# Two output projections as three products of split operands, and one pool of twelve for the ring's slots

## The chip, the cores and the metric

The kernel runs on one core of one Trainium2 chip, in one launch. The metric is the device time of that launch in microseconds. The core's engines run side by side, each through its own list of instructions in order: TensorE (PE, with its weight loads as PEld), VectorE (DVE), ScalarE (ACT), GpSimd (POOL) and SyncE (SP), which here issues nearly all the transfers from the chip's memory.

## The reference, cut to what matters

A two-layer network on 256 tokens of width 1024. Layer 0 mixes tokens by attention, layer 1 by a Hyena convolution; each mixer ends in an output projection, and a mixture of 16 experts follows it. Modulation vectors (`mod_w`, 40 MB) scale and shift around all of this.

```
def attention_group_mixer(...):          # layer 0
    ...
    def merge(oa, ow):
        ...
        cat = jnp.concatenate([oa..., ow...], -1)
        return cat @ w_out               # [256,1024] @ [1024,1024]

def hyena_mixer(h, w_in, ...):           # layer 1
    u = h @ w_in
    ...
        z = gate * (conv + zf32 * sk[o]).astype(h.dtype)
    return z @ w_out                     # [256,1024] @ [1024,1024]

def moe_ffn(h, router_w, router_bias, w_gate, w_up, w_down):
    scores = jax.nn.softmax(hf @ router_w)
    ...                                  # best group of 4, two experts a token
    def expert_block(args):
        xb, e = args
        return (jax.nn.silu(xb @ w_gate[e]) * (xb @ w_up[e])) @ w_down[e]
```

All inputs are float32.

## The kernel before, in words

**Weights and the ring.** Every weight tile is 1 MB, [128, 2048] float32. Twelve slots of that size, w0 to w11, make the ring; `slots["order"]` hands them out by turns, so each load has its slot fixed when the program is written, and waits until that slot's last reader is done. From the end of each mixer to the end of its experts there are also `MORE[l]` extra slots (4 in layer 0, 5 in layer 1). `load` (L146) issues every tile on SP's queue, in program order, with at most eight under way.

**Stages.** Layer 0's mixer streams the modulation weights beside attention. `mixer_tail` then runs: it loads the mod vector g1b and the first tiles of expert 0 into the extra slots, `project` (L427) multiplies mixT (or z2T in layer 1) by the four tiles of `out_weights`, `normalize` (L435, L436, L361, L375) adds the residual and takes the layer norm, `logits` (L445 to L453) transposes it and scores the experts, and a chain of small DVE steps makes the routing tables. `project` accumulates token half t in two PSUM banks, one for each 512 columns; a float32 matmul of 512 columns shows as two records in the trace.

**Experts.** `moe` takes the positions p = 0 to 9 in order: `up` (L648), `turn_mid` (L657), `down` (L667), `back` (L686), with two large experts as dense pieces (L711, L723) between p = 1 and 8. An expert needs 12 tiles: four pairs of gate and up, and four of down. At p = 9 (`NEST`) the kernel first loads eight tiles of expert 9 into ring slots of their own, then enters nested conditionals (`rare`, L761) for the experts at positions 10 to 13, which run only where the routing needs them, with the other slots; after them it loads expert 9's last four tiles and runs it.

**The end.** After layer 1's experts the kernel adds the last term, takes a layer norm (L1409, L1410) and stores the output.

**Split operands.** `split` writes `hi`, a rounded copy (ACT), and `lo`, the difference (DVE), as float32r; the Hyena input products (L1296) for five of six column blocks already use hi·hi, hi·lo and lo·hi in place of one float32 product.

Of the kernel before, what the change touches and what calls it, by code (L numbers as in the profile page):

```python
# [75 lines left out]
def emit(tc, I, O):  # L76
# [3 lines left out]

    with es:
        cp = es.enter_context(tc.tile_pool(name="cp", bufs=1))
        ring = es.enter_context(tc.tile_pool(name="ring", bufs=1))
        accp = es.enter_context(tc.tile_pool(name="accp", bufs=1, space=PSUM))
        miscp = es.enter_context(tc.tile_pool(name="miscp", bufs=1, space=PSUM))
        dram = es.enter_context(tc.tile_pool(name="dram", bufs=1, space=DRAM))
# [15 lines left out]
                mturn[0] ^= 1  # L102
            return miscp.tile([128, 512], F32, name=f"mis{i}", tag=f"mis{i}")

        slots = {"order": list(range(RING)), "at": 0}

        def wtile(i=None):

            if i is None:
                i = turns()[0]  # L110
                slots["at"] += 1
            return (ring if i < RING else slots["pool"]).tile([128, 2048], F32, name=f"w{i}", tag=f"w{i}")

        def turns(order=None):

            if order is None:
                a = slots["at"] % len(slots["order"])
                return slots["order"][a:] + slots["order"][:a]
            slots["order"], slots["at"] = order, 0

        def more_ring(l):

# [4 lines left out]
            return xp, pool_  # L127

        def all_slots(n):
            turns(turns() + [RING + i for i in range(n)])  # L130

        def less_ring(pool_):
            turns([i for i in turns() if i < RING])
            for p_ in pool_:
                p_.__exit__(None, None, None)

        def load(src, shape, slot=None):
            t = wtile(slot)
            v = t
            n = 1  # L140
            for s in shape:
                n *= s
            v = t[:, :n]
            if len(shape) == 2:
                v = v.rearrange("p (a b) -> p a b", a=shape[0])
            sp.dma_start(out=v, in_=src)  # L146
            return v
# [249 lines left out]
            dve.tensor_tensor(out=b, in0=b, in1=sh, op=ALU.add)  # L397

        def out_weights(src):
            return [load(src[256 * i:256 * i + 256, :].rearrange("(k p) n -> p k n", p=128), [2, 1024]) for i in range(4)]  # L400


        def stage_h2():
# [2 lines left out]
        def mixer_tail(l, stage, mixT, wout, R):  # L406
# [15 lines left out]
                pe.matmul(lg[0:16, 256:257], rw[:, kc, :], cb[:, kc:kc + 1], start=(kc == 0), stop=(kc == KC - 1))  # L422
            dve.tensor_copy(lcol[0:16, :], lg[0:16, 256:257])

            def project(t, banks, kh):
                for kc, hf in kh:
                    m = pe.matmul(banks[hf], mixT[:, kc, 128 * t:128 * t + 128], wout[kc // 2][:, kc % 2, 512 * hf:512 * hf + 512],  # L427
                                  start=(kc == 0), stop=(kc == KC - 1))
                return m.ins

            def normalize(t, banks):
# [142 lines left out]
        def expert_loads(l, idx, have=(), most=12, new=False):  # L574

            def src(nm, i):
                return expert_of(l, nm, idx)[256 * i:256 * i + 256, :].rearrange("(k p) f -> p k f", p=128)

            order = [(nm, i) for i in range(4) for nm in ("exp_w_gate", "exp_w_up")] + [("exp_w_down", i) for i in range(4)]
            ts = list(have)  # L580
            for nm, i in order[len(ts):]:
                ts.append(load(src(nm, i), [2, 1024], slot=RING + len(ts) if new else None))
                if len(ts) == most:
                    break
            return ts
# [144 lines left out]
        def moe(l, h2, R, first, filler):  # L730
            with tc.tile_pool(name=f"mp{l}", bufs=2, reuse_waits="tile") as mp:
# [73 lines left out]
                for p in range(RARE):  # L805
                    if p == NEST:

                        ix = number(1, place(p), [ET.SP], NE - 1)
                        w = expert_loads(l, ix, most=8)
                        last.back()  # L810
                        last = None
                        free = turns()
                        own, free = free[-8:], free[:-8]
                        turns(free)
                        rare(RARE)
                        E.bank = E.banks()
                        free.sort(key=lambda i: i < RING)
                        turns(free[:4])
                        E.w = expert_loads(l, ix, have=w)
                        turns(free[4:] + own + free[:4])  # L820
                    elif p == 0:
                        E.w = first
                    else:
                        ix = number(1, place(p), [ET.SP], NE - 1) if p > 1 else 1
                        E.w = expert_loads(l, ix, have=second if p == 1 else (), most=8)
                        if p in PIECES:
                            r, half, down = PIECES[p]
                            dw = dense_loads(l, number(1, 2 + r, [ET.SP], NE - 1), half, down)
                        E.w = expert_loads(l, ix, have=E.w)
                    E.up()  # L830
                    if last:
# [403 lines left out]
                if i + 1 < len(oq):  # L1235
                    spec_loads(*oq[i + 1])

        def win_tile(s, i):
            return load(wi[512 * i:512 * i + 512, 512 * s:512 * s + 512].rearrange("(k p) n -> p k n", p=128), [4, 512])

        with tc.tile_pool(name="fp", bufs=1, reuse_waits="tile", side="right") as fp:
            wi = I["hy_w_in"][0]
            moe(0, h2, R, first, filler)
            ws0 = [win_tile(j // 2, j % 2) for j in range(NAHEAD)]
        less_ring(rmore)

        R = routing_tables()
# [227 lines left out]
```

## Time and profile before

| | |
|---|---|
| median of 3 runs | 1320.58 us (1314.1 to 1323.14) |
| profiled execution | 1321.82 us, span 1320.1 us |
| mean granted TensorE clock | 0.946 |
| PE busy | 1177.6 us (89%) |
| DVE busy | 550.0 us (42%) |
| ACT busy | 216.6 us (16%) |
| moved by DMA | 443.88 MB, 336 GB/s on average |

The time of an execution is 1.7 us longer than its span here. A busy share is an average over stages: the same engine can be the limit in one stage and idle in the next, so each stage is read for itself.

### The profile page before, as it was taken

What the parts mean: (1) busy time and instruction counts of PE and PEld (TensorE: products, weight loads), DVE (VectorE), ACT (ScalarE), POOL (GpSimd) and SP (SyncE); (2) the same over time, 40 slices, a digit from 0 to 9 for tenths busy, and PEclk for the clock granted to TensorE, in tenths of its full rate; (3) what the DMA queues carried; (4) which work ended last, traced back from release to release, by engine and by line L of the source; (5) the groups of instructions that cost most, each with busy time, mean ns of one, the idle gap of its engine ahead of it and who ended that gap; (6) DMA issues with size and microseconds to landing.
All of it is one profiled execution on the core that took longest, in us unless ns stands there. A gap on an engine that the chain in (4) does not pass through costs nothing. (4 is left out here: it accounts for less than half of the span.)

```text
span 1320.1 us, 19948 instructions
## 1 busy us (share of the span) xinstructions
PE 1177.6 (89%) x8106; PEld 700.8 (53%) x8106; DVE 550.0 (42%) x1131; ACT 216.6 (16%) x431; POOL 48.4 (4%) x88
## 2 busy tenths in 40 slices
PE   5999989978999999999776779899799999999994
PEld 2444545434845648466432348675366465574842
DVE  2467998374122141321421157995530312313033
ACT  2133546130000000000000025321210000000000
POOL 1000000211000000000100010000100000000000
PEclk9999998978999999999977789899799999999998
DMA  9978986869599799999999794368499999999994
GB/s 329 397 287 318 336 328 234 319 260 394 217 405 405 267 397 405 408 398 392 398 395 409 275 372 159 127 225 334 180 393 408 401 390 359 402 374 402 408 383 160
DMA packets 133207, 443.88 MB, mean 336 GB/s; under 512 B 8271, under 2 KB 9895, under 8 KB 133104
## 3 DMA queue, kind: packets, MB, share of 16 engines
q1 hardware_dynamic: 127168, 426.76, 83.7%
q0 software_dynamic: 4864, 13.18, 2.9%
q10 hardware_dynamic: 1072, 2.54, 0.6%
q8 instruction: 68, 1.11, 0.3%
q14 instruction: 35, 0.29, 0.1%
HBM read 437.19 MB, written 5.26 MB: 335 GB/s over the span
## 5 line engine op out<-in xcount | busy, mean ns | idle before, releaser
L648 PE MATMUL acc<-w,xe 128*32 128x256 f32 (+1 forms) x2688 | 216.7, 428 | 17.9 <-PEq L761 7.4
L711 PE MATMUL acc<-xnT,w 128*128 128x256 f32 x1024 | 222.8, 379 | 0.4 <-DVE xs L692 0.4
L711 PEld LDWEIGHTS acc<-xnT,w 128*128 128x128 f32 x1024 | 194.3, 190 | 26.7 <-DVE xs L692 0.6
L648 PEld LDWEIGHTS acc<-w,xe 128*32 128x32 f32 (+1 forms) x2688 | 102.6, 120 | 121.4 <-issue 68.1
L667 PE MATMUL acc<-w,aT 128*32 128x256 f32 (+1 forms) x1344 | 120.2, 426 | 9.7 <-DMA w<-in_exp_w_down 3.9
L723 PE MATMUL acc<-w,hid 128*128 128x512 f32 x256 | 111.5, 593 | 0.3 <-DVE xs L692 0.3
L714 DVE TENSOR_TENSOR hid<-hid,acc 128x256 f32<-128x256 f32 x32 | 13.4, 420 | 190.4 <-ACT hid L713 190.4
L271 DVE SCALAR_TENSOR_TENSOR w<-w,cz,w 128x1024 f32<-128x1024 f32 x60 | 75.0, 1277 | 22.7 <-DMA w<-in_mod_w 22.6
L667 PEld LDWEIGHTS acc<-w,aT 128*32 128x32 f32 (+1 forms) x1344 | 48.4, 117 | 66.9 <-issue 30.0
L723 PEld LDWEIGHTS acc<-w,hid 128*128 128x128 f32 x256 | 48.0, 190 | 58.6 <-issue 57.6
L692 DVE TENSOR_TENSOR xs<-xs,acc 128x512 f32<-128x512 f32 x92 | 57.6, 683 | 47.1 <-PE acc L686 47.1
L652 DVE TENSOR_TENSOR ac<-ac,acc 128x256 f32<-128x256 f32 (+1 forms) x23 | 10.7, 467 | 148.3 <-PE acc L648 148.3
L943 PE MATMUL acc<-w,hT 128*128 128x512 f32 (+1 forms) x192 | 71.5, 523 | 0.9 <-DVE mr L166 0.8
L1296 PE MATMUL acc<-hTh,w 128*128 128x256 f32 x320 | 63.0, 293 | 5.4 <-DVE w L155 3.7
L1296 PEld LDWEIGHTS acc<-hTh,w 128*128 128x128 f32 x320 | 50.2, 190 | 9.7 <-DVE w L155 4.4
L725 DVE SCALAR_TENSOR_TENSOR do<-acc,wtP,g2b 128x512 f32<-128x512 f32 x32 | 24.0, 751 | 69.7 <-PE acc L723 69.7
L943 PEld LDWEIGHTS acc<-w,hT 128*128 128x128 f32 x192 | 35.4, 190 | 32.4 <-issue 29.2
L651 ACT ACTIVATE ac<-acc 128x256 f32<-128x256 f32 (+1 forms) x23 | 9.7, 420 | 254.9 <-PE acc L648 254.9
L616 PE MATMUL mis<-h,Pu 128*32 128x256 f32 (+1 forms) x336 | 38.1, 470 | 13.8 <-DVE Pu L610 9.9
L686 PE MATMUL acc<-xg,PT 32*128 32x256 f32 (+1 forms) x336 | 41.2, 434 | 6.0 <-DVE xg L672 4.6
L713 ACT ACTIVATE hid<-acc 128x256 f32<-128x256 f32 x32 | 12.3, 383 | 208.7 <-PE acc L711 208.7
L1296 PE MATMUL acc<-hTl,w 128*128 128x256 f32 x160 | 45.1, 283 | 0.0
(351 smaller groups left out, 1272.9 us busy)
## 6 DMA issues: line engine op xcount, KB each, us to landing
w<-in_exp_w_up SPq DMA_DIRECT2D x108, 1024.0 KB, 17.8
w<-in_exp_w_gate SPq DMA_DIRECT2D x108, 1024.0 KB, 17.7
w<-in_exp_w_down SPq DMA_DIRECT2D x108, 1024.0 KB, 10.8
w<-in_mod_w SPq DMA_DIRECT2D x40, 1024.0 KB, 9.6
w<-in_hy_w_in SPq DMA_DIRECT2D x12, 1024.0 KB, 13.8
w<-in_attn_w_in SPq DMA_DIRECT2D x9, 1024.0 KB, 13.1
w<-in_mod_w SPq DMA_DIRECT2D x16, 512.0 KB, 10.8
w<-in_attn_w_out SPq DMA_DIRECT2D x4, 1024.0 KB, 13.4
```

The source lines that it names most:

```text
L271: dve.scalar_tensor_tensor(out=st["acc"][:, k], in0=w[:, k], scalar=c_[k], in1=st["acc"][:, k], op0=ALU.mult, op1=ALU.add)
L616: pe.matmul(gb[S * j:S * j + S, 0:nn], Pu[:, t, 0:S], self.h2[:, t, nn * j:nn * j + nn], start=(t == 0), stop=(t == 1), tile_position=(0, ...
L648: pe.matmul(A[m][S * j:S * j + S, 0:nn], self.xe[:, kc, :], w[:, nn * j:nn * j + nn], tile_position=(0, S * j), start=(kc == 0), stop=(kc ...
L667: pe.matmul(y[S * q:S * q + S, 0:nn], lhs, w[:, nn * q:nn * q + nn], tile_position=(0, S * q), start=(kc == 0), stop=(kc == KC - 1))
L686: pe.matmul(o, self.PT[r, 128 * t:128 * t + 128], self.yb[r, 0:nn], start=True, stop=True, tile_position=(S * q, 0))
L692: dve.tensor_tensor(out=x_, in0=x_, in1=o, op=ALU.add)
L711: pe.matmul(b[:, N * m:N * m + N], ws[m][kc // 4][:, kc % 4, 128 * fb:128 * fb + 128], h2T[:, kc, :], start=(kc == 0), stop=(kc == KC - 1))
L714: dve.tensor_tensor(out=hid[:, fb, :], in0=hid[:, fb, :], in1=b[:, N:2 * N], op=ALU.mult)
L723: pe.matmul(b, hid[:, fb, 128 * t:128 * t + 128], ws[fb // 2][:, fb % 2, s_], start=(fb == 0), stop=(fb == 3))
L725: dve.scalar_tensor_tensor(out=o, in0=b, scalar=wt[:, t], in1=g2b[:, s_], op0=ALU.mult, op1=ALU.mult)
L943: pe.matmul(bank[:, 0:width], hT[:, kc, 128 * t:128 * t + 128], st["w"][kc // per][:, kc % per, :], start=(kc == 0), stop=(kc == KC - 1))
L1296: pe.matmul(b[:, 0:N], w_, m, start=(kc == 0 and i == 0), stop=(kc == KC - 1 and i == len(ps) - 1))
```

## The change

`out_weights` still loads four tiles, but each is split into a hi and a lo tile that take two more slots from the ring; mixT or z2T is split the same way, in four pieces, into mixH and mixL; `project` makes three float32r products for each block where it made one of float32. The ring becomes one pool of twelve buffers: a load takes whichever buffer the pool gives it. For expert 9 only `MORE[l]` tiles (4 in layer 0, 5 in layer 1) are loaded ahead of the conditionals, into the extra slots, so that the conditional experts have all twelve ring buffers; its other 8 (layer 0) or 7 (layer 1) tiles are loaded behind them.

```diff
@@ ring
-        ring = es.enter_context(tc.tile_pool(name="ring", bufs=1))
+        ring = es.enter_context(tc.tile_pool(name="ring", bufs=RING))
...
-            return (ring if i < RING else slots["pool"]).tile([128, 2048], F32, name=f"w{i}", tag=f"w{i}")
...
+                slots["turn"] = (slots["turn"] + 1) % (RING + slots["more"])
+                i = slots["turn"] - RING
+            if i < 0:
+                return ring.tile([128, 2048], F32, name="w", tag="w")
+            return slots["pool"].tile([128, 2048], F32, name=f"w{i}", tag=f"w{i}")
@@ out_weights
-            return [load(src[256 * i:256 * i + 256, :].rearrange("(k p) n -> p k n", p=128), [2, 1024]) for i in range(4)]
+
+            o = []
+            for i in range(4):
+                w = load(src[256 * i:256 * i + 256, :].rearrange("(k p) n -> p k n", p=128), [2, 1024])
+                hi, lo = (wtile().rearrange("p (k n) -> p k n", k=2) for _ in range(2))
+                for k in range(2):
+                    split(w[:, k], hi[:, k], lo[:, k])
+                o.append((hi, lo))
+            return o
@@ mixer_tail
+            mixH, mixL = (stage.tile([128, KC, N], F32, name=nm, tag=nm) for nm in ("mixH", "mixL"))
+            for t in range(2):
+                for c0 in range(0, KC, 4):
+                    v = mixT[:, c0:c0 + 4, 128 * t:128 * t + 128]
+                    split(v, mixH[:, c0:c0 + 4, 128 * t:128 * t + 128], mixL[:, c0:c0 + 4, 128 * t:128 * t + 128])
+
             def project(t, banks, kh):
                 for kc, hf in kh:
-                    m = pe.matmul(banks[hf], mixT[:, kc, 128 * t:128 * t + 128], wout[kc // 2][:, kc % 2, 512 * hf:512 * hf + 512],
-                                  start=(kc == 0), stop=(kc == KC - 1))
+                    wh, wl = (r_(w[:, kc % 2, 512 * hf:512 * hf + 512]) for w in wout[kc // 2])
+                    mh, ml = (r_(v[:, kc, 128 * t:128 * t + 128]) for v in (mixH, mixL))
+                    for i, (a_, b_) in enumerate(((mh, wh), (mh, wl), (ml, wh))):
+                        m = pe.matmul(banks[hf], a_, b_, start=(kc == 0 and i == 0), stop=(kc == KC - 1 and i == 2))
                 return m.ins
@@ moe, p == NEST
-                        w = expert_loads(l, ix, most=8)
+                        w = expert_loads(l, ix, most=MORE[l], new=True)
                         last.back()
                         last = None
-                        free = turns()
-                        own, free = free[-8:], free[:-8]
-                        turns(free)
                         rare(RARE)
                         E.bank = E.banks()
-                        free.sort(key=lambda i: i < RING)
-                        turns(free[:4])
                         E.w = expert_loads(l, ix, have=w)
-                        turns(free[4:] + own + free[:4])
...
+                        if p + 1 == NEST:
+                            all_slots(0)
                         E.w = expert_loads(l, ix, have=E.w)
@@ hyena
-            ws0 = [win_tile(j // 2, j % 2) for j in range(NAHEAD)]
+            ws0 = [win_tile(j // 2, j % 2, -1) for j in range(NAHEAD)]
```

In the changed kernel's lines `load` is L142, `split`'s subtraction L151, `project` L440, `normalize` L447, `logits` from L457.

Order on PE at the end of layer 0's projection, before: acc_1591 and acc_1592 are the banks of token half 0, acc_1593 and acc_1594 those of half 1.

```order
L427 MATMUL acc_1591<-w_1551,mixT 128x512
L427 MATMUL acc_1592<-w_1551,mixT 128x512
L427 MATMUL acc_1593<-w_1545,mixT 128x512 x2
L427 MATMUL acc_1593<-w_1547,mixT 128x512 x2
L427 MATMUL acc_1593<-w_1549,mixT 128x512 x2
L427 MATMUL acc_1593<-w_1551,mixT 128x512 x2
L427 MATMUL acc_1594<-w_1545,mixT 128x512 x2
L427 MATMUL acc_1594<-w_1547,mixT 128x512 x2
L427 MATMUL acc_1594<-w_1549,mixT 128x512 x2
L427 MATMUL acc_1594<-w_1551,mixT 128x512 x2
L445 MATMUL mis_1642<-blob,h_1573 128x128 x4
```

The same place after; acc_1625 and acc_1626 are half 0, acc_1627 and acc_1628 half 1.

```order
L440 MATMUL acc_1625<-w,mixH 128x512
L440 MATMUL acc_1625<-w,mixL 128x512
L440 MATMUL acc_1626<-w,mixH 128x512
L440 MATMUL acc_1626<-w,mixL 128x512
L440 MATMUL acc_1627<-w,mixH 128x512
L440 MATMUL acc_1627<-w,mixL 128x512
L440 MATMUL acc_1627<-w,mixH 128x512 x2
L440 MATMUL acc_1627<-w,mixL 128x512
L440 MATMUL acc_1628<-w,mixH 128x512
L440 MATMUL acc_1628<-w,mixL 128x512
```

Half 0 was finished sixteen matmuls (32 records) ahead of the end; now it is finished twelve float32r matmuls ahead, the halves running side by side.

Order on DVE where Hyena ends and layer 1's projection begins, before: x2c is the gated branch, z2T the projection's input.

```order
L1301 SCALAR_TENSOR_TENSOR x2c<-acc_6344,ccol,x2c 128x255
L1301 SCALAR_TENSOR_TENSOR x2c<-acc_6372,ccol,x2c 128x255
L1362 TENSOR_TENSOR z2T<-acc_6409,x2c 128x2x128
L1362 TENSOR_TENSOR z2T<-acc_6415,x2c 128x2x128
...
L1362 TENSOR_TENSOR z2T<-acc_6445,x2c 128x2x128
L1362 TENSOR_TENSOR z2T<-acc_6451,x2c 128x2x128
L417 MEMSET rws 128x256
L420 MEMSET lcol 128x1
L418 TENSOR_TENSOR rws<-rw,fold 128x8x16
L423 COPY lcol<-acc_6481 16x1
L435 TENSOR_TENSOR lnr_6496<-acc_6498,g1b 128x512
```

The same place after.

```order
L151 TENSOR_TENSOR w<-w 128x1024
L1309 SCALAR_TENSOR_TENSOR x2c<-acc_6470,ccol,x2c 128x255
L151 TENSOR_TENSOR w<-w 128x1024
L1370 TENSOR_TENSOR z2T<-acc_6531,x2c 128x2x128
...
L151 TENSOR_TENSOR w<-w 128x1024 x2
L421 MEMSET rws 128x256
L424 MEMSET lcol 128x1
L151 TENSOR_TENSOR mixL<-z2T,mixH 128x4x128
L422 TENSOR_TENSOR rws<-rw,fold 128x8x16
L427 COPY lcol<-acc_6603 16x1
L151 TENSOR_TENSOR mixL<-z2T,mixH 128x4x128 x3
L151 TENSOR_TENSOR w<-w 128x1024 x4
```

Twelve subtractions have come in: two ahead of the eight z2T steps, ten behind them.

Order on SP behind layer 1's conditionals (L761 before, L773 after), before: the tiles of expert 9, then the output.

```order
L761 UNCONDITIONAL_BRANCH x4
...
L146 DMA w_9938<-in_exp_w_down 128x2x1024
...
L146 DMA w_9940<-in_exp_w_down 128x2x1024
...
L146 DMA w_9942<-in_exp_w_down 128x2x1024
...
L146 DMA w_9944<-in_exp_w_down 128x2x1024
L1414 DMA out<-xs 128x1024
```

And after.

```order
L773 UNCONDITIONAL_BRANCH x4
...
L142 DMA w<-in_exp_w_up 128x2x1024
...
L142 DMA w<-in_exp_w_gate 128x2x1024
...
L142 DMA w<-in_exp_w_up 128x2x1024
...
L142 DMA w<-in_exp_w_down 128x2x1024
...
L142 DMA w<-in_exp_w_down 128x2x1024
```

Seven transfers stand behind the branch (the three above and four of w_down) where four stood.

## Rows read from the trace of the kernel before

**Rows 1.** Windows by stage: busy us (instructions) of each engine, PE clock, DMA share, GB/s.
```profile
360.00:660.00 300.00, 288.56 (x2042) 170.24 (x2034) 84.47 (x170) 16.78 (x41) 10.87 (x18) 0.99 0.99 387
660.00:745.00 85.00, 59.24 (x678) 27.45 (x682) 13.34 (x35) 3.45 (x9) 0.00 (x0) 0.75 0.96 381
787.00:906.00 119.00, 110.20 (x700) 91.74 (x699) 103.61 (x147) 48.63 (x78) 1.21 (x3) 0.95 0.56 203
906.00:956.00 50.00, 40.26 (x184) 19.07 (x185) 22.42 (x85) 10.17 (x22) 4.15 (x8) 0.86 0.63 234
956.00:1289.00 333.00, 320.81 (x2470) 196.00 (x2462) 87.55 (x177) 18.93 (x44) 0.00 (x0) 1.00 0.99 389
1289.00:1320.00 31.00, 14.25 (x210) 8.60 (x210) 11.35 (x22) 2.64 (x5) 0.00 (x0) 0.79 0.45 170
```

**Rows 2.** PE in order of time, projection and tail of layer 0.
```profile
238.25 21.62 PE L427 MATMUL acc<-w,mixT 128*128 128x512 f32 x50
260.52 1.11 PE L445 MATMUL mis<-blob,h 128*128 128x128 f32 x8 [0.64 <-DVE h L375]
...
278.16 2.36 PE L648 MATMUL acc<-w,xe 128*32 128x256 f32 x20 [0.92 <-DVE xe L633]
```

**Rows 3.** Groups by line: duration ns min/median/max, first and last start us.
```profile
L427 PE MATMUL acc<-w,z2T x64: 592/592/697, 906.3 to 933.4; 128*128 128x512 f32 x64
L154 ACT ACTIVATE w<-w x20: 1037/1046/1063, 791.6 to 892.9; 128x1024 fp32r<-128x1024 f32 x20
L155 DVE TENSOR_TENSOR w<-w,w x20: 1214/1218/1226, 793.0 to 894.2; 128x1024 fp32r<-128x1024 f32 x20
L164 ACT ACTIVATE tmp<-mis x16: 577/597/599, 132.7 to 235.1; 128x512 f32<-128x512 f32 x16
```

**Rows 4.** PE in order of time, float32r products and float32 products of 256 columns.
```profile
896.27 0.39 PE L1296 MATMUL acc<-hTh,w 128*128 128x256 f32 x2
896.50 0.28 PE L1296 MATMUL acc<-hTl,w 128*128 128x256 f32 x1
896.62 0.51 PE L1296 MATMUL acc<-hTh,w 128*128 128x256 f32 x3
...
1223.43 27.79 PE L711 MATMUL acc<-xnT,w 128*128 128x256 f32 x128
```

**Rows 5.** DVE in order of time, normalization behind the projection of layer 0.
```profile
259.92 1.00 DVE L375 TENSOR_SCALAR h<-lnr,mv,rs 128x512 f32<-128x512 f32 x2 [4.72 <-PE acc L427]
260.84 0.68 DVE L435 TENSOR_TENSOR lnr<-acc,g1b 128x512 f32<-128x512 f32 x1
...
263.90 1.00 DVE L375 TENSOR_SCALAR h<-lnr,mv,rs 128x512 f32<-128x512 f32 x2
```

**Rows 6.** DVE in order of time, end of the Hyena stage, and layer 1's normalization.
```profile
896.61 2.36 DVE L1341 TENSOR_TENSOR Y<-ms,md 128x1024 f32<-128x1024 f32 x2
...
905.93 0.43 DVE L1362 TENSOR_TENSOR z2T<-acc,x2c 128x256 f32<-128x256 f32 x1 [0.47 <-PE acc L1358]
...
938.09 1.00 DVE L375 TENSOR_SCALAR h<-lnr,mv,rs 128x512 f32<-128x512 f32 x2
```

**Rows 7.** PE in order of time, conditional experts and expert 9, layer 0.
```profile
744.79 1.15 PE L686 MATMUL acc<-xg,PT 32*128 32x256 f32 x16 [0.56 <-DVE xg L672]
749.66 9.36 PE L648 MATMUL acc<-w,xe 128*32 128x256 f32 x128 [3.73 <-PEq L761]
...
767.61 3.48 PE L1212 MATMUL acc<-fwo,hs 128*128 128x256 f32 x8 [3.11 <-DMA fwo<-in_hy_ffn_w_out]
```

**Rows 8.** SP in order of time, transfers of expert 9, layer 1.
```profile
1253.49 0.38 SPq L146 DMA_DIRECT2D w<-in_exp_w_gate  x1
...
1289.06 3.27 SPq L146 DMA_DIRECT2D w<-in_exp_w_down  x4
```

**Rows 9.** The chain that ended last, in order of time from its start.
```profile
1291.95 11.43 DMA w<-in_exp_w_down
...
1303.43 1.11 PE acc L667 x16
```

More of the change, by code (lines that the diff above doesn't have):

```diff
@@ L103, in mbank @@
             return miscp.tile([128, 512], F32, name=f"mis{i}", tag=f"mis{i}")
-        slots = {"order": list(range(RING)), "at": 0}
+        slots = {"turn": RING - 1, "more": 0}
         def wtile(i=None):
             if i is None:
-                i = turns()[0]
-                slots["at"] += 1
-            return (ring if i < RING else slots["pool"]).tile([128, 2048], F32, name=f"w{i}", tag=f"w{i}")
[L114 to L119, printed above, removed]
+                slots["turn"] = (slots["turn"] + 1) % (RING + slots["more"])
[3 more added lines that the diff above has]
+            return slots["pool"].tile([128, 2048], F32, name=f"w{i}", tag=f"w{i}")
         def more_ring(l):
@@ L129, in all_slots @@
         def all_slots(n):
-            turns(turns() + [RING + i for i in range(n)])
+            slots["more"] = n
+            slots["turn"] = RING + n - 1
         def less_ring(pool_):
-            turns([i for i in turns() if i < RING])
+            all_slots(0)
             for p_ in pool_:
@@ L581, in expert_loads @@
             for nm, i in order[len(ts):]:
-                ts.append(load(src(nm, i), [2, 1024], slot=RING + len(ts) if new else None))
+                ts.append(load(src(nm, i), [2, 1024], slot=len(ts) if new else None))
                 if len(ts) == most:
@@ L828, in moe @@
                             dw = dense_loads(l, number(1, 2 + r, [ET.SP], NE - 1), half, down)
+                        if p + 1 == NEST:
+                            all_slots(0)
                         E.w = expert_loads(l, ix, have=E.w)
@@ L1236, in filler, with win_tile @@
                     spec_loads(*oq[i + 1])
-        def win_tile(s, i):
-            return load(wi[512 * i:512 * i + 512, 512 * s:512 * s + 512].rearrange("(k p) n -> p k n", p=128), [4, 512])
+        def win_tile(s, i, slot=None):
+            return load(wi[512 * i:512 * i + 512, 512 * s:512 * s + 512].rearrange("(k p) n -> p k n", p=128), [4, 512], slot=slot)
         with tc.tile_pool(name="fp", bufs=1, reuse_waits="tile", side="right") as fp:
```

## The prediction, made before the changed kernel ran

> **What bounds the kernel now.** I read the windows by stage first, then the chain of waits at the end, then PE and DVE in order of time around the places that the diff touches. The expert stages are bound by transfers: the DMA engines are 0.99 busy from 360 to 660 and from 956 to 1289, and 0.96 through layer 0's conditional experts, where PE is idle 30% of the time and its granted clock falls to 0.75 [rows 1]. The Hyena stage is bound by DVE, 103.6 us busy of 119, with PE close behind [rows 1]. Between a mixer and its experts stands a chain that transfers don't set: projection on PE, normalization on DVE, logits and routing; from 238.25 to the first expert matmul at 278.16 in layer 0 [rows 2]. The end of the kernel hangs on a transfer: expert 9's four tiles of w_down are issued at 1289.06, the last lands at 1303.38, and its sixteen matmuls start 0.05 us later [rows 8, 9]. So four places decide: the two tails, the conditionals of layer 0, Hyena, and the end.
>
> **The projection on PE.** Before, layer 1 runs 64 records from 906.3 to 933.4 plus the last one's 0.59, 27.7 us [rows 3]; 50 records in 21.62 us in layer 0 give a pitch of 0.432 us [rows 2]. Such a record is half a float32 product. Nothing in this trace shows a float32r product of 512 columns. At 256 columns the float32r product has a pitch of 0.35 us for three, 0.117 us [rows 4], and the float32 record 27.79/128 = 0.217 us [rows 4]; so one float32r product costs 1.08 of half a float32 record. Carried over to 512 columns that is between 0.432/2 = 0.216 and 0.234 us. I take 0.224, the middle. Ends for the range: 0.117 (it costs as at 256 columns), 0.432 (as a float32 record). 96 products x 0.224 = 21.5 us, against 27.7: PE saves 6.2 us a layer if nothing else moves.
>
> What this row allows speaks against a rule. In the Trainium skill, TensorE: Matmul & The Clock Gate, section Back-to-back issue gap, a sustained stream of weight load and 512-column matmul is put at about 131 ns each; by that 96 products would take 12.6 us. The pitch of 0.117 us at half the columns [rows 4] leaves no room for 0.131 at all of them, so the sum doesn't use it; it stands as part of a rival below.
>
> **Layer 0's tail.** Before, 14 of the 64 records ran in the gaps of the window attention and only 50 stand behind it, 21.62 us [rows 2]. By the new order all 96 stand behind the attention, since the first needs mixH, and mixH the last pieces of mixT. So 21.5 us replaces 21.62, and ahead of it come a copy on ACT (0.6 us [rows 3]) and, on DVE, two weight subtractions of 1.22 us [rows 3] among the steps that end the attention: the projection ends 0 to 3 us later, I take 0.7. The rest of the splits, 8 copies and 8 subtractions of the weights and 4 of each for mixT, about 13 us on each engine, have the projection and the attention's gaps beside them; if their tiles come late that cover is gone and each costs its 1.22 us. Then the order of the banks: before, half 0 was normalized while half 1 ran, and behind the end stood half 0's last step and half 1's chain, up to 263.90 + 1.00, that is 5.0 us after 259.9 [rows 5]. Now half 0's banks are finished 12 products, 2.7 us, before the end, and some 17 DVE steps of both halves, 0.69 us for the wide ones and 1.0 for the two last pairs [rows 5], stand behind that: about 7.8 us after the end. Cost 2.8 us. Layer 0's tail: +3.5 us (-3 to +8).
>
> **Layer 1's tail.** z2T is the end of a DVE stretch with hardly a gap from 896.61 on [rows 6]. Two weight subtractions now stand inside it: +2.4 us. Two more, 2.4 us, stand between z2T and the first mixL, and PE has 8 products (1.8 us) that need no mixL: it waits about 1 us. Of the saving of 6.2, 2.8 remains; the order of the banks takes 2.8 more (before, half 1's last pair ends at 939.1, 5.0 us after the projection [rows 6]), and ACT's copy ahead of the first product 0.6. Layer 1's tail: about +0.8 us (-5 to +6).
>
> **First tiles of the experts.** Twelve ring buffers now hold the split weights where four slots did, so expert 0's ring tiles queue on SP behind w_out tiles and wait for subtractions and for the projection's progress. Twelve tiles at 2.7 us (1.05 MB at the 389 GB/s of [rows 1]) are 32 us; the tail lasts 40 us [rows 2] and the same window of layer 1 moves only 234 GB/s [rows 1]. I cost it at nothing; the cover is this slack of 8 us, and each tile beyond it costs 2.7.
>
> **Layer 0's conditionals.** SP issues four tiles fewer ahead of them. That stretch is transfer-bound [rows 1], so it ends 4 x 2.75 = 11 us earlier (381 GB/s there). But behind it eight tiles must come where four did, 11 us more, after a restart of 3.73 us in which PE finds nothing [rows 7]. The last w_down lands about when it did. Expert 9's up runs under these loads instead of ahead of them, and the filter work that follows, which waited 3.11 us for its own weights [rows 7], starts earlier. I take -4 us (-8 to +3).
>
> **Hyena.** Its tiles now come in program order into whichever buffer is free. DVE was idle for 15 of 119 us [rows 1]; at most a part of that can go, and a wrong order can add as much. I take -1 us (-6 to +4).
>
> **The end.** No conditional expert runs in layer 1: the last eight tiles ahead of the branch are issued from 1253.49 on, and SP next issues at 1289.06 [rows 8], after PE has finished expert 8. Five tiles instead of eight ahead of the branch only lengthen the idle time of the DMA engines, since PE is the limit there and expert 8's own tiles come first. Behind it come seven instead of four: three more at 2.7 us, +8.1 us, straight onto the chain, as expert 9's first 80 matmuls and the two other gate and up tiles are hidden under the wait. A rule bears on the size alone: the Trainium skill, DMA: Bandwidth & Descriptors, section Specifications, gives a limit of about 358 GB/s from memory for one core; by it the three tiles would cost 8.8 us. The 389 GB/s over 333 us [rows 1] is above that, and the measurement decides.
>
> **Sum.** +3.5 + 0.8 - 4 - 1 + 8.1 = +7.4 us on the profiled execution's own 1321.82, so 1329.2; the median of the three runs lies 1.2 below that execution, so I predict 1328 us.
>
> **Rivals.** (1) *The projection's saving comes through.* If DVE keeps up and the banks' order costs nothing, each tail gains 6 us, and with -8 in the conditionals, -4 in Hyena and +8.1 at the end it is 1305 to 1308. For it: PE is the named limit of the projection, DVE waited 4.72 us for it [rows 5]. Against: the fourteen records that were free, and DVE's place on the path before z2T. By the skill's 131 ns, named above, each tail would gain 9 us more and the end would be near 1290; the 0.117 us pitch makes that under 1 in 30, and it is inside this case. (2) *Slower: the experts start hungry.* SP's queue is in order, so one w_out tile that waits for a buffer holds all of expert 0's ring tiles. For it: those waits now hang on subtractions and on projection rows. Against: 8 us of slack. It decides when the first ring tile is issued more than 8 us into the projection; if five tiles are late in each layer it costs 13 us a layer, 1341 to 1354. (3) *The late loads cost nothing*: SP passes layer 1's branch as soon as its own transfers are out, some 15 us before 1289. Then the 8.1 goes, 1320. For it: SP itself waits for nothing but a number. Against: the four tiles before were issued only at 1289.06 [rows 8], though their slots belonged to tiles long used. This is also the case in which the change does nothing that shows.
>
> **How the numbers follow.** Forecast 0.52, rival 1 0.13, rival 2 0.20, rival 3 0.15. About 1% (13 us) is what a measurement of this kernel can tell from no change; that puts the borders at 1307 and 1334. The forecast's own spread, mostly the tails, is 1316 to 1338, a fifth of it above 1334. Faster: most of rival 1 and a little of the others, 0.14. Slower: rival 2 and that fifth, with a part of it for tails that are worse than summed, 0.30. Same: 0.56. The range reaches from the edge of rival 1 to the lower half of rival 2: 1308 to 1346.
>
> **What would show it.** In the changed kernel's trace: 96 records of L440 a layer with a pitch near 0.224 us; the last pair of L371 about 7.8 us behind the last of them; a z2T that ends about 2.4 us later against the Hyena stage's start; seven transfers behind layer 1's branch, the last landing some 22 us after the first is issued, and L679's last sixteen matmuls waiting for it. It is wrong if that landing is no later than before, if the experts' first matmuls wait for gate or up tiles, or if PE's granted clock in a projection is at the lower of its levels.

## The result and the profile after

The changed kernel takes 1330.4 us (median of 4 runs, 1329.06 to 1332.67); the kernel before, beside it, 1317.44 us (1314.1 to 1323.14). The ratio is 1.0091, 95% interval 1.0065 to 1.0118: slower, by something under 1%. Beside the experiments the kernel before was run 20 to 30 times a set and has 1320 to 1321; against that the change costs 0.7 to 0.8%. The profiled execution took 1332.67 us, its span 1330.6 us at a mean granted clock of 0.943, 10.5 us longer than the span before.

Seven stretches, cut at the same instructions in both traces (starts and ends of PE and DVE rows in order of time), show where the 10.5 us are. "First expert matmul" is L648 before and L660 after, "dense" L711 and L723, "back" L686 and L698.

| stretch, us | before | after | difference |
|---|---|---|---|
| 1 start to layer 0's first expert matmul | 278.2 | 276.7 | -1.5 |
| 2 to the end of layer 0's last back | 499.9 | 494.2 | -5.7 |
| 3 to the last z2T written | 128.2 | 126.6 | -1.6 |
| 4 to layer 1's first expert matmul | 46.7 | 41.5 | -5.2 |
| 5 to layer 1's first dense piece | 26.8 | 42.4 | +15.6 |
| 6 to the end of expert 8's back | 305.9 | 306.3 | +0.4 |
| 7 to the end of the span | 34.4 | 42.9 | +8.5 |

Stretches 1 to 4 gain 14.0 us, 5 and 7 lose 24.1. PE of the changed kernel in order of time, at the borders and in the projections:

```profile
231.18 0.97 PE L440 MATMUL acc<-w,mixH 128*128 128x512 f32 x3 [0.30 <-ACT mixH L150]
...
246.95 0.63 PE L440 MATMUL acc<-w,mixH 128*128 128x512 f32 x2
247.42 0.39 PE L440 MATMUL acc<-w,mixL 128*128 128x512 f32 x1
247.65 0.63 PE L440 MATMUL acc<-w,mixH 128*128 128x512 f32 x2
...
253.71 0.40 PE L440 MATMUL acc<-w,mixL 128*128 128x512 f32 x1
258.75 1.94 PE L457 MATMUL mis<-blob,h 128*128 128x128 f32 x8 [4.64 <-DVE h L371]
...
276.73 8.49 PE L660 MATMUL acc<-w,xe 128*32 128x256 f32 x112 [0.92 <-DVE xe L645]
...
732.91 1.15 PE L698 MATMUL acc<-xg,PT 32*128 32x256 f32 x16 [0.56 <-DVE xg L684]
...
921.15 0.39 PE L440 MATMUL acc<-w,mixL 128*128 128x512 f32 x1
...
938.99 9.32 PE L660 MATMUL acc<-w,xe 128*32 128x256 f32 x128 [0.92 <-DVE xe L645]
...
957.13 0.69 PE L669 MATMUL acc<-blob,ac 128*128 128x128 f32 x2 [6.73 <-DVE ac L664]
...
981.40 0.81 PE L723 MATMUL acc<-xnT,w 128*128 128x256 f32 x3
```

Three products from 246.95 to 247.65 are a pitch of 0.233 us, and the first starts 7.1 us earlier than the series of [rows 2]. The new wait is at 957.13: PE had ended expert 0's first half, and the selection of the next expert's tokens, and stood for 6.73 us. DVE in order of time says why, and GpSimd's queue what it waited for:

```profile
260.89 1.00 DVE L371 TENSOR_SCALAR h<-lnr,mv,rs 128x512 f32<-128x512 f32 x2
...
914.81 1.40 DVE L447 TENSOR_TENSOR lnr<-acc,g1b 128x512 f32<-128x512 f32 x2 [4.49 <-PE acc L440]
...
924.74 1.00 DVE L371 TENSOR_SCALAR h<-lnr,mv,rs 128x512 f32<-128x512 f32 x2
...
953.18 2.36 DVE L846 TENSOR_TENSOR xs<-h,hid 128x1024 f32<-128x1024 f32 x2 [8.29 <-DMA hid<-in_ln_g]
```

```profile
934.64 0.53 POOL L1409 DMA_DIRECT2D gbf<-in_ln_g  x1 [157.49 <-DVE r_ws L544]
935.17 0.53 POOL L1409 DMA_DIRECT2D gbf<-in_ln_b  x1
935.69 0.53 POOL L348 DMA_DIRECT2D g2b<-mdram  x1
936.21 2.00 POOL L747 DMA_DIRECT2D g2r<-mdram  x4
938.20 0.57 POOL L348 DMA_DIRECT2D hid<-in_ln_g  x1
```

The row ln_g is issued at 938.20 and lands 15.0 us later. Windows of the changed kernel around it (columns as in [rows 1]) show a DMA share of about 1.0 from 900 on, after a Hyena end that moved little:

```profile
880.00:890.00 10.00, 8.00 (x70) 7.81 (x68) 10.00 (x14) 3.59 (x5) 0.00 (x0) 1.00 0.28 107
...
900.00:910.00 10.00, 9.29 (x41) 7.51 (x41) 7.05 (x12) 3.21 (x4) 0.00 (x0) 1.00 0.99 394
...
940.00:950.00 10.00, 9.43 (x142) 4.77 (x135) 4.89 (x20) 2.05 (x3) 1.08 (x2) 0.82 1.03 392
950.00:960.00 10.00, 2.80 (x22) 1.25 (x24) 6.82 (x14) 0.38 (x1) 0.00 (x0) 0.69 1.03 405
```

In the kernel before, the tile view of that row's transfers (two, one for each layer) reads

```profile
DMA to landing us min/median/max: 4.1/4.2/4.3
```

and in the changed kernel

```profile
DMA to landing us min/median/max: 6.0/10.5/15.0
```

so a transfer that took 4.3 us at most before (in layer 1 from 944.46 to 948.61, beside a mean DMA share of 0.73) takes 15.0 among weights.

That wait is not all of stretch 5. Cut at expert 0's turn (L657 before, L669 after) and at the next expert's first up matmul, it is 12.3, 4.3 and 10.2 us before and 18.1, 5.8 and 18.5 us after. The first part has the wait. In the second, PE's granted clock averages 0.70 behind the stand (a mean over both of its levels, 1.2 and 2.4 GHz), against 1.00 before. In the third, PE's list is another one. Before, 154 records stand ahead of the dense piece:

```profile
969.64 7.09 PE L648 MATMUL acc<-w,xe 128*32 128x256 f32 x128
976.66 1.15 PE L686 MATMUL acc<-xg,PT 32*128 32x256 f32 x16
977.74 1.94 PE L616 MATMUL mis<-h,Pu 128*64 128x512 f32 x8
979.61 0.44 PE L657 MATMUL acc<-blob,ac 128*128 128x128 f32 x2
```

After, the same 154 stand there cut into pieces, and with them 14 more that select and turn the tokens of later experts. Two of the pieces and some of these selections:

```profile
968.44 1.07 PE L660 MATMUL acc<-w,xe 128*32 128x256 f32 x16
...
972.11 0.55 PE L640 MATMUL mis<-blob,xg 128*128 128x128 f32 x3 [0.74 <-ACT xg L160]
...
974.72 1.93 PE L628 MATMUL mis<-h,Pu 128*64 128x512 f32 x6 [0.59 <-DVE PT L162]
976.58 1.07 PE L660 MATMUL acc<-w,xe 128*32 128x256 f32 x16
```

PE stands for 1.9 us in this part. No wait of PE in stretch 5 names a weight tile. No line of the change names these steps; why their order came out otherwise is not shown.

The end, SP's transfers of expert 9 and the chain that ended last, beside [rows 8, 9]:

```profile
1258.61 0.38 SPq L142 DMA_DIRECT2D w<-in_exp_w_gate  x1
...
1290.57 0.39 SPq L142 DMA_DIRECT2D w<-in_exp_w_up  x1
1291.31 1.21 SPq L142 DMA_DIRECT2D w<-in_exp_w_gate  x1
1292.77 0.37 SPq L142 DMA_DIRECT2D w<-in_exp_w_up  x1
1293.35 2.07 SPq L142 DMA_DIRECT2D w<-in_exp_w_down  x4
```

```profile
1295.05 17.05 DMA w<-in_exp_w_down
...
1312.14 1.98 PE acc L679 x16
```

Seven transfers, issued from 1290.57 and landed at 1312.10, 21.5 us, where four took 14.3.

### The profile page after: what moved, and what is told of

Its sections match the earlier page's. It is cut to its first block, busy times and chain, and to the rows that moved or that the text cites. A ratio compares the mean times of both kernels' runs of the same rounds, so it can differ in the third digit from the quotient of the medians.

```text
span 1330.6 us, 20147 instructions
## 1 busy us (share of the span) xinstructions
PE 1171.0 (88%) x8170; PEld 712.1 (54%) x8170; DVE 571.7 (43%) x1155; ACT 234.7 (18%) x455; POOL 48.4 (4%) x88
## 5 line engine op out<-in xcount | busy, mean ns | idle before, releaser
L660 PE MATMUL acc<-w,xe 128*32 128x256 f32 (+1 forms) x2688 | 224.6, 431 | 19.2 <-PEq L773 7.1
L723 PE MATMUL acc<-xnT,w 128*128 128x256 f32 x1024 | 222.3, 379 | 0.0
L723 PEld LDWEIGHTS acc<-xnT,w 128*128 128x128 f32 x1024 | 194.3, 190 | 25.6
L660 PEld LDWEIGHTS acc<-w,xe 128*32 128x32 f32 (+1 forms) x2688 | 102.4, 120 | 126.9 <-issue 72.9
L679 PE MATMUL acc<-w,aT 128*32 128x256 f32 (+1 forms) x1344 | 112.1, 422 | 11.1 <-DMA w<-in_exp_w_down 6.9
L267 DVE SCALAR_TENSOR_TENSOR w<-w,cz 128x1024 f32<-128x1024 f32 x60 | 75.7, 1289 | 10.9 <-DMA w<-in_mod_w 10.9
L1304 PE MATMUL acc<-hTh,w 128*128 128x256 f32 x320 | 59.9, 286 | 0.0
L698 PE MATMUL acc<-xg,PT 32*128 32x256 f32 (+1 forms) x336 | 46.4, 446 | 5.0 <-DVE xg L684 5.0
L725 ACT ACTIVATE hid<-acc 128x256 f32<-128x256 f32 x32 | 12.3, 383 | 207.8 <-PE acc L723 207.8
L160 ACT ACTIVATE xg<-mis 128x256 f32<-128x256 f32 (+1 forms) x23 | 9.7, 420 | 221.8 <-PE mis L628 118.1
## 6 DMA issues: line engine op xcount, KB each, us to landing
w<-in_exp_w_up SPq DMA_DIRECT2D x108, 1024.0 KB, 17.1
```

The source lines that it names most:

```text
L267: dve.scalar_tensor_tensor(out=st["acc"][:, k], in0=w[:, k], scalar=c_[k], in1=st["acc"][:, k], op0=ALU.mult, op1=ALU.add)
L660: pe.matmul(A[m][S * j:S * j + S, 0:nn], self.xe[:, kc, :], w[:, nn * j:nn * j + nn], tile_position=(0, S * j), start=(kc == 0), stop=(kc ...
L679: pe.matmul(y[S * q:S * q + S, 0:nn], lhs, w[:, nn * q:nn * q + nn], tile_position=(0, S * q), start=(kc == 0), stop=(kc == KC - 1))
L698: pe.matmul(o, self.PT[r, 128 * t:128 * t + 128], self.yb[r, 0:nn], start=True, stop=True, tile_position=(S * q, 0))
L723: pe.matmul(b[:, N * m:N * m + N], ws[m][kc // 4][:, kc % 4, 128 * fb:128 * fb + 128], h2T[:, kc, :], start=(kc == 0), stop=(kc == KC - 1))
L1304: pe.matmul(b[:, 0:N], w_, m, start=(kc == 0 and i == 0), stop=(kc == KC - 1 and i == len(ps) - 1))
```

## The experiments

Two theories at the start. **A**: transfers set both losses; the three more tiles behind the branch cost the end, and the split weights keep expert 0's tiles out of the ring during Hyena, so that the first dense piece of layer 1 waits for tiles. **B**: the loss at the experts' start is DVE's wait for the ln_g row and not the tiles, and the end has another cause. The profiled executions, cut as above:

| stretch, us | 1 | 2 | 3 | 4 | 5 | 6 | 7 |
|---|---|---|---|---|---|---|---|
| before | 278.2 | 499.9 | 128.2 | 46.7 | 26.8 | 305.9 | 34.4 |
| after | 276.7 | 494.2 | 126.6 | 41.5 | 42.4 | 306.3 | 42.9 |
| e1 keep3 | 279.6 | 495.6 | 129.2 | 42.4 | 42.2 | 306.3 | 34.2 |
| e2 layer 1 f32 | 278.5 | 494.1 | 125.6 | 46.0 | 25.8 | 305.4 | 42.1 |
| e3 ln rows first | 276.0 | 493.1 | 125.7 | 42.1 | 32.1 | 306.2 | 42.3 |
| e4 down once | 275.0 | 493.9 | 125.5 | 42.1 | 35.8 | 311.6 | 41.7 |
| e5 before, five | 276.9 | 499.4 | 128.1 | 46.7 | 25.3 | 305.9 | 41.6 |
| e6 before, split | 279.3 | 498.5 | 136.8 | 41.3 | 26.4 | 305.7 | 34.0 |
| e7 pool, f32 | 270.4 | 494.3 | 125.4 | 45.6 | 25.3 | 305.8 | 42.2 |
| e8 keep3, layer 1 f32 | 279.5 | 493.8 | 126.2 | 46.0 | 26.0 | 305.9 | 33.6 |
| e9 f32, keep3 | 278.4 | 493.0 | 126.2 | 46.0 | 26.0 | 305.6 | 33.8 |
| e10 split, keep3, ln | 282.1 | 494.4 | 129.8 | 41.8 | 31.8 | 308.7 | 34.2 |
| e11 pool alone | 277.6 | 499.6 | 126.1 | 46.0 | 26.1 | 305.9 | 34.8 |
| e12 f32, keep3, ln | 278.2 | 490.3 | 126.6 | 46.0 | 26.1 | 305.9 | 34.5 |

**e1 keep3.** Eight tiles ahead of layer 1's branch again; three ring slots get names of their own, so that the conditional experts can't be given them.

```diff
+            if i < -3:
+                return ring.tile([128, 2048], F32, name="w", tag="w", bufs=RING - 3)
             if i < 0:
-                return ring.tile([128, 2048], F32, name="w", tag="w")
+                return ring.tile([128, 2048], F32, name=f"k{-i}", tag=f"k{-i}", bufs=1)
...
-                        w = expert_loads(l, ix, most=MORE[l], new=True)
+                        w = expert_loads(l, ix, most=8 if l else MORE[l], new=True)
```

> The changed kernel, but in layer 1 eight tiles of expert 9 are loaded ahead of the conditionals as before: five in the extra slots and three in ring slots taken out of the pool for them. Theory A (the end is longer because three more tiles come behind the branch): four transfers behind the branch, the last landing about 14 us after the first issue instead of 22, last chain 8 us shorter, total 1322. Rival B (the last expert waits for something else, or SP's passage through the branch is later by as much): the end stays at about 43 us behind expert 8, total 1330.

Measured: 1332.18 us, ratio 1.0094 (1.0057 to 1.0131). The stretch that was in question did what A said, 42.9 to 34.2 us, with four transfers behind the branch (SP in order of time):

```profile
1279.19 2.21 SPq L146 DMA_DIRECT2D k<-in_exp_w_up  x1
1298.45 3.52 SPq L146 DMA_DIRECT2D w<-in_exp_w_down  x4
```

The total did not follow. Stretches 1 to 4 lost 7.8 us. The edit also leaves a pool of nine and three slots by turns; that this is the cost is argued here, and e9 and e11 come back to it. A's cause for the end stands, its forecast of the total fell.

**e2 layer 1 float32.** Layer 1's projection as before, on four ring slots; layer 0's still split.

```diff
         def out_weights(src, l):
+            if l:
+                return [load(src[256 * i:256 * i + 256, :].rearrange("(k p) n -> p k n", p=128), [2, 1024]) for i in range(4)]
```

> The changed kernel, but layer 1's projection is the float32 one, with four ring slots and no split. Theory A (layer 1's shorter tail is worth nothing, since the first dense piece of the experts waits for transfers that start later): the first expert matmul starts some 5 us later against the end of the Hyena stage, the first dense piece starts no later than in the changed kernel, total 1330 within 4, rather below. Rival B (the lead is lost to DVE's wait for the ln_g row): the tail's 5 to 6 us pass through, total 1336.

Measured: 1315.32 us, ratio 0.9976 (0.9954 to 0.9998). The tail is 4.5 us longer, as both said; the first dense piece comes 16.6 us sooner behind the first expert matmul. Stretches 4 and 5 together fall from 83.9 to 71.8, below the 73.5 of before. B's 1336 is out, and A's total is 15 us too high: the split in layer 1 didn't gain nothing, it cost 12 us.

**e3 ln rows first.** GpSimd issues ln_g and ln_b ahead of the g2 rows, and the final norm's rows behind.

```diff
+                lng = row_bc(mp, I["ln_g"][l, 0:1, :], "hid", pool)
+                lnb = [...]
                 g2b = mod_bc(mp, l, 1, "g2b", pool)
...
-                lng = row_bc(mp, I["ln_g"][l, 0:1, :], "hid", pool)
```

> The changed kernel, but GpSimd issues the rows ln_g and ln_b of the experts' stage ahead of the g2 rows, and the final norm's rows behind them. Both theories: DVE's wait of 8.3 us for ln_g and the 6.7 us in which PE is idle after expert 0's first half shrink to 2 us or less. Theory A (transfers set the first dense piece): it starts within 2 us of where it did, total 1330 within 3. Rival B (that wait sets it): it starts 5 to 7 us earlier, total 1324.

Measured: 1315.78 us, ratio 0.9978 (0.9956 to 1.0). PE in order of time, with no wait behind expert 0's first half:

```profile
936.85 8.49 PE L660 MATMUL acc<-w,xe 128*32 128x256 f32 x128 [0.92 <-DVE xe L645]
...
948.07 0.38 PE L669 MATMUL acc<-blob,ac 128*128 128x128 f32 x2
...
968.95 3.40 PE L723 MATMUL acc<-xnT,w 128*128 128x256 f32 x15
```

Stretch 5 is 10.3 us shorter with the same tiles in the same order: B for the larger part of the 15.6 us. Its three parts are 11.2, 4.3 and 16.6 us, so 6.9 come from the wait, 1.4 from the clock behind it and 2.0 from the third part. The row itself still took 7.1 us; it was issued 17.1 us ahead of the first expert matmul instead of 0.8. The edit also takes the 1 MB of the final norm's rows out of this place, and no run tells that from the order. Stretch 5 is 32.1 still, against 25 to 27 in the kernels whose layer 1 is not split or whose ring goes by turns: all of the rest is the third part, in which PE has the longer list (168 records) and stands for 1.2 us, for no tile.

**e4 down once.** Expert 0 of layer 1 loads one tile of w_down in place of four.

```diff
-            first = expert_loads(l, 0, have=early)
+            first = expert_loads(l, 0, have=early, most=9 if l else 12)
+            first += [first[8]] * (12 - len(first))
```

> The changed kernel, but in layer 1 expert 0 loads one tile of w_down and uses it in place of all four, so that a part of the computation is changed and three transfers of 1 MB are left out at the start of the experts. Theory A (transfers set the first dense piece): it starts about 8 us earlier against the first expert matmul, total 1322. Rival B (the wait for ln_g sets it): at most the 2 to 3 us by which that row lands earlier, total 1328.

Measured: 1327.26 us, ratio 1.006 (1.0034 to 1.0086). DVE still waits for the row:

```profile
950.56 2.36 DVE L847 TENSOR_TENSOR xs<-h,hid 128x1024 f32<-128x1024 f32 x2 [8.15 <-DMA hid<-in_ln_g]
```

The first dense piece is 6.6 us earlier, near A's 8, but not for A's reason: the first two parts of stretch 5 are no shorter together than in the changed kernel (18.0 and 6.6 us), and the third is 11.1 us because PE's list is here the short one of 154 records. Stretch 6 gives 5.3 back, more than in any other run (e10 has 2.4 more than the changed kernel, the rest are within 1 us of it). From z2T to expert 8's back it is 389.5 us against 390.2. Fewer tiles at the start are worth next to nothing; this speaks for B. The time that the transfers save turns up as time in which the DMA engines stand. The changed kernel's stretch 6, and 20 us of it from 180 us behind the last z2T on (columns as in [rows 1]):

```profile
981.40:1287.73 306.33, 296.67 (x2114) 181.42 (x2112) 70.17 (x136) 15.63 (x38) 0.00 (x0) 1.00 0.96 376
1077.50:1097.50 20.00, 20.00 (x95) 17.64 (x94) 1.26 (x3) 1.15 (x3) 0.00 (x0) 1.00 0.40 142
```

and the same place of this run:

```profile
1074.50:1094.50 20.00, 20.00 (x94) 17.64 (x93) 1.27 (x3) 1.15 (x3) 0.00 (x0) 1.00 0.13 47
```

PE is busy throughout while the DMA engines stand for more than half of the time. No wait of PE in stretch 6 names a weight tile, here, in the changed kernel or in the kernel before, while SP's loads wait for PE, in the changed kernel 71.1 us in all for the matmuls of L723 (970 to 1285). So PE, not the transfers, sets the time of stretch 6.

**e5 before, with five.** The kernel before with five tiles of expert 9 ahead of layer 1's conditionals and seven behind.

```diff
-                        w = expert_loads(l, ix, most=8)
+                        own_n = 5 if l else 8
+                        w = expert_loads(l, ix, most=own_n)
```

> The kernel before, with one edit: in layer 1 five tiles of expert 9 are loaded ahead of the conditionals and seven behind them. Theory A (each tile behind the branch costs its transfer): +8 us at the end and nothing elsewhere, ratio to before 1.006, about 1325. Rival B: the five leave room for other transfers ahead of the branch, or the branch is passed earlier, ratio 1.000.

Measured: 1328.57 us, ratio 1.0061 (1.0039 to 1.0083). Stretch 7 is 7.2 us longer, all others within 1.5: of the end's 8.5 us, 7.2 come from the three tiles alone.

**e6 before, with split projections.** The changed `out_weights`, the split of mixT and the three products in the kernel before; ring by turns, eight tiles ahead.

> The kernel before, ring by turns and eight tiles of expert 9 ahead of the conditionals, but with the projections as three float32r products. Theory A: the end is that of before (34 us behind expert 8), layer 1's tail is shorter by some 5 us, and the start of layer 1's experts takes back what the tail gave, since the split weights keep expert 0's tiles out of the ring: ratio 1.000, within 0.004. Rival B (the projections give and only the end takes): ratio 0.99, about 1306.

Measured: 1325.33 us, ratio 1.0042 (1.0022 to 1.0063). B is out. A's total is near its edge for another reason than it gave: stretch 5 is as short as before, and stretch 3, Hyena, pays 8.6 us. Its waits of PE there name

```profile
PE acc L1374 <- DVE z2T L1378: 5.2, 1, 5.2
```

a wait that the kernel before has not. Where the price falls depends on who hands out the slots; there is a price in both.

**e7 pool, float32.** Both projections float32, the pool and the conditionals as changed (the changed kernel with the old `out_weights` and `project`).

> The changed kernel, but both projections are float32 ones without a split; pool and conditionals as changed. Theory A: layer 1's first dense piece starts no later than in the changed kernel although the tail is longer; conditionals of layer 0 and the end are as changed; total 1328 to 1332. Rival B (the projections' gain passes through): 6 us more a layer, 1340.

Measured: 1311.32 us, ratio 0.9943 (0.9914 to 0.9971). Faster than either theory allowed, as stretch 1 is 6 us shorter too. ACT's last copy of mixT starts at 236.91 in the kernel before, 230.33 in the changed one and, in this one,

```profile
230.26 0.28 ACT L160 ACTIVATE mixT<-mis 128x128 f32<-128x128 f32 x1 [1.26 <-PE mis L1059]
```

so the pool ends the attention 6.6 us earlier. From there to the first expert matmul it is 40.2 us here, 41.3 before and 46.4 with the split.

**e8 keep3 and layer 1 float32.** The edits of e1 and e2 together.

> The changed kernel with float32 projection in layer 1 and eight tiles of expert 9 ahead of layer 1's conditionals, three of them in kept ring slots. Theory A: layer 0's conditionals keep their gain of 5 to 7 us, the start of layer 1's experts is that of before, the end is that of before: total 1312 to 1316, at or just below the kernel before. Rival B: 1322 or more.

Measured: 1314.05 us, ratio 0.9961 (0.9942 to 0.9981); as expected, stretch by stretch (2, 4, 5 and 7).

**e9 float32 and keep3.** e7 with e1's edit.

> Float32 projections in both layers, the pool, four tiles of expert 9 ahead of layer 0's conditionals, eight ahead of layer 1's (three in kept ring slots). If the pieces measured so far add up, the end gives 8 us on the 1311.3 of the run with float32 projections and seven late tiles: 1303, ratio 0.987. If the nine-slot pool costs what layer 0's mixer showed in two runs with kept slots (2 to 3 us later), 1306.

Measured: 1310.51 us, ratio 0.9914 (0.9887 to 0.9941). Stretch 7 gives 8.4 us, stretch 1 takes 8.0: the second expectation was right in its cause and too small in its size. Ahead of the end of stretch 1 this kernel differs from e7's by the ring alone, nine slots in the pool and three by turns.

**e10 the change, repaired.** e1's and e3's edits in the changed kernel.

> The changed kernel with split projections in both layers, eight tiles of expert 9 ahead of layer 1's conditionals and the ln rows ahead of the g2 rows. If the two repairs add up: 1315.8 less 8, 1308, ratio 0.991. If the kept slots cost 2 to 3 us in layer 0's mixer, 1311.

Measured: 1320.34 us, ratio 1.0009 (0.9994 to 1.0024). Both repairs show in 5 and 7 (31.8 and 34.2); stretch 1 is 282.1, the longest of all, and 1 to 3 together are 8.8 us above the changed kernel. Even so repaired, the split leaves the kernel where it was before, 14.7 us behind the same kernel with float32 projections (e12).

**e11 pool alone.** Float32 projections, eight tiles ahead in both layers; four kept slots.

> Float32 projections, the pool, but eight tiles of expert 9 ahead of the conditionals in both layers (four and three of them in kept ring slots): the ring's change alone. If the pool hands layer 0's mixer its 7 us: first expert matmul at 270 to 273 instead of 277 to 278. If the four tiles ahead of the conditionals were what shortened layer 0's experts by 5.6 us, that stage is back at 499 to 500 us here; if the pool was, it stays at 494. Total 1308 by the first pair, 1304 by the second.

Measured: 1318.05 us, ratio 0.9978 (0.9957 to 0.9999). Stretch 2 is 499.6: the 5.6 us of layer 0's experts come from the four tiles ahead of the conditionals, not from the pool. Stretch 1 is 277.6, and ACT's last copy of mixT stands at

```profile
236.39 0.28 ACT L164 ACTIVATE mixT<-mis 128x128 f32<-128x128 f32 x1 [1.24 <-PE mis L1065]
```

where the kernel before has it. It stands at 229.0 to 232.8 in the five kernels with all twelve slots in one pool (the changed one, e2, e3, e4, e7) and at 233.6 to 238.8 in the nine others, so the attention's gain needs the whole pool.

**e12 float32, keep3, ln rows.** e9 with e3's edit.

> As the float32 run with three kept slots, with the ln rows ahead of the g2 rows as well. With float32 projections the start of layer 1's experts was already 25 to 26 us from first expert matmul to first dense piece, so if the rows only matter where transfers are dense there, nothing changes: within 2 us of that run. If the rows were late in every kernel, 3 to 6 us less.

Measured: 1305.69 us, ratio 0.9891 (0.9856 to 0.9925). Stretches 4 and 5 are those of e9, so the rows don't matter where the start isn't dense with transfers. The 2.7 us in stretch 2 may come from layer 0's rows, which the edit moves too, or from the spread between executions; the intervals of e9 and e12 overlap. It is the fastest that was run.

## Why the prediction was right, and where it wasn't

The time was forecast at 1328 and measured at 1330.4, slower and within 1%. That the sum came so near is luck: its terms for stretches 1 to 4 add up to -0.7 us, where -14.0 was measured, and stretch 5, put at nothing, cost 15.6.

- **The end, +8.1: right in its cause, its size partly by luck.** Measured +8.5, and shown by e5 (put in alone, +7.2) and e1, e8 to e12 (taken out, 33.6 to 34.8 in all). Rival 3, that late loads cost nothing, is out. The three tiles cost 7.2 us from first issue to last landing (21.5 against 14.3), 2.4 each where 2.7 was taken. Behind the landing 1.8 more came in: the last 32 records of PE ran at a granted clock of 0.50 (the lower level, 1.2 GHz) after PE had stood for tiles, at 1.00 before; the sixteen of w_down took 1.98 us instead of 1.11 [rows 9]. SP's first issue came 0.5 us sooner behind expert 8. The limit of about 358 GB/s in the Trainium skill, DMA: Bandwidth & Descriptors, section Specifications, would by an estimate have made the three tiles 8.8; the 7.2 measured lies below that.
- **Layer 0's conditionals, -4: right, a little small.** Measured -5.7, and e11 shows the cause. The last conditional expert's back starts 10.4 us sooner against the first expert matmul (466.6 before, 456.2 after), near the 11 that were worked out; the eight tiles behind take back 4.7 of it, not 11.
- **Hyena, -1: right way.** Measured -1.6. Stretch 3 is 128.1 and 128.2 in the two kernels with the old ring and float32 projections and 125.4 to 126.6 in nine of the pool's; the two with kept slots and a split layer 1 (e1, e10) lose it again.
- **The product's pitch, 0.224: right in its range.** It is 0.233, the upper end that was scaled from the 256 columns. The 131 ns of the Trainium skill, TensorE: Matmul & The Clock Gate, section Back-to-back issue gap, is not seen here; that section's formula for a single matmul would give 216, nearer to the measured 233.
- **Layer 0's tail, +3.5: right way, too small.** From ACT's last mixT to the first expert matmul the split costs 5.2 us (46.4 against 41.3; e7, without it, 40.2). The order of the banks came as worked out: the last pair ends 7.8 us behind the last product (261.89 against 254.11). The series of products was longer by 1.3 us, and 1.6 us more went between that pair and the first expert matmul.
- **Stretch 1 as a whole: a term was missing.** The prediction had the tail's cost and no gain ahead of it. The pool ends the attention 6.6 us sooner, which the split then takes back.
- **Layer 1's tail, +0.8: wrong way.** Its own steps add up to +0.6; measured -5.2. The projection gave 4.0 us (23.7 against 27.7). The two subtractions ahead of z2T cost nothing that shows in stretch 3, and the order of the banks cost nothing either: DVE began half 0's norm 6.7 us before the last product ended (914.81 against 921.54), and the last pair ended 4.2 us behind it, where it was 5.1 before. That term had been carried over from layer 0 without reading layer 1's order.
- **The first tiles, at nothing: the step that failed.** The cover named, 8 us of slack for the tiles, did not matter, since PE waited for no weight tile in stretch 5. What came late was one row of 0.5 MB on another engine's queue, ln_g. It took 15.0 us instead of 4.1 and cost 7.3 of the 15.6 us, the wait and the lower clock behind it; e3's edit gives 10.3 back. The other 8.3 us are the longer list of PE ahead of the dense piece, 14 records more and the rest in pieces. It stands in the kernels with the pool and a split layer 1, except e4, and in no other; its cause is not shown. Stretch 6 did not become shorter by the work that was done ahead of it. With the row repaired, the whole way from z2T to expert 8's back is 380.4 us with the split (e3) and 377.6 without it in layer 1 (e2), so there the tail's saving is more than taken back.
- **What bounds the experts: read from the wrong column.** The prediction took the DMA share of 0.99 in [rows 1] for the limit. The same row has PE busy 320.81 of 333 us, and the waits and e4 show that PE sets the time of stretch 6.
- **Rival 1** was half true: the saving came through in layer 1's tail. **Rival 2** named the place where it was lost, but its cause, tiles that come late, is not what PE waited for.

The split by itself is a loss. With both repairs the kernel stands at 1.0009 of before (e10), and the same kernel without the split at 0.9891 (e12), 14.7 us less; without the repairs it is 1330.4 against 1311.3 (e7). What remains open is a kernel with a full pool of twelve, float32 projections and eight tiles ahead of layer 1's branch; that wasn't run, since the conditional experts need slots that expert 9 doesn't hold.

## What to carry to other kernels

A saving on one engine is paid out only if everything that the next stage needs comes as early as before. Here 5 us saved in a tail came with a denser queue, in which a small row that nobody counted took 11 us longer and held VectorE, and with it PE. So list the small transfers on every queue beside the place that is changed, and put those that are needed first ahead of those that are needed last. A DMA share near 1 does not make transfers the limit: look whether the engine waits for tiles or the loads wait for buffers. And compare the order of an engine's list before and after, since a change can move work that its lines do not touch. In this kernel each tile put behind the branch cost 2.4 us there: count the tiles on each side of it.

## What the runs showed of the hardware that was not expected

A float32r product of 512 columns has a pitch of 0.233 us, twice the 0.117 of 256 columns [rows 4], where a float32 record of 512 columns has 0.432 [rows 2]. A transfer of 0.5 MB on GpSimd's queue took 4.1 us from issue to landing beside a DMA share of 0.73 and 15.0 us beside one of 1.03; the Trainium skill, DMA: Bandwidth & Descriptors, section Queues, rings and completion order, says that the engines take the queues in turn, packet by packet, and such a stretch under load is what one would see by it. No run here tells it from the rows issued ahead of it on the same queue. Three kernels with the same layer 0 as the changed one, or one that differs behind stretch 1 alone (e2, e3, e4), ended stretch 1 at 275.0 to 278.5 us, so a single profile does not settle 3 us there.
